# State-space rounds: two buffers for the cosine and sine tables, angles rounded on ScalarE one step sooner, two more chunks of the strips kept for the last round

## The chip, the cores and the metric

One Trainium2 chip, one core of it. The metric is the device time of one execution in microseconds (us). The kernel before was run three times; its time is the median. One more execution was recorded with the hardware profiler, and every row of the profile shown here is from that execution.

The engines are called as the profile calls them: PE (TensorE matmuls), PEld (its weight loads), DVE (VectorE), ACT (ScalarE), POOL (GpSimd) and SP (SyncE, which only starts transfers). The names with a q (SPq, ACTq, PEq) are the queues of instructions that start transfers or wait on semaphores.

## The reference, cut to what matters

A two-layer decoder trunk for 1024 tokens of width 1024, in float32. Layer 0 is a block-diagonal state-space mixer, layer 1 a forgetting attention. The change touches only the state-space mixer of layer 0:

```python
u, z = jnp.split(h @ w_in, 2, axis=-1)
abar = exp(ar*dt) * (cos(ai*dt) + i sin(ai*dt))        # 64 groups x 64 states
ug = u.reshape(bsz, L, 64, 16)                         # 64 groups of 16 channels
bu = einsum('blgc,gpc->blgp', ug, bb)                  # complex input of the states
s  = associative_scan(s_t = abar * s_{t-1} + bu_t)     # over the 1024 tokens, complex
y  = einsum('blgp,gcp->blgc', s_r, C_re) - einsum('blgp,gcp->blgc', s_i, C_im)
y  = gelu(y.reshape(bsz, L, 1024) + D * u)
y  = y * sigmoid(y @ w_glu + b_glu) * silu(z)
x  = x + gate * (y @ w_out)
```

## The kernel before, in words

**Layout of the scan.** Eight tokens make a chunk, so the scan runs over 128 chunks. The 64 groups are taken in eight rounds e = 0 to 7 of eight groups. A state tile is 128 partitions (64 real parts above 64 imaginary parts, or the reverse) by 8 groups by 128 chunks, which is 128x1024 in the profile. The complex recurrence is made real by turning the states by the angle of chunk k: the input is multiplied by cosine and sine (tables `cT` and `sT`), a real scan follows with a decay, and the result is turned back with the same tables.

**The functions of a round.**
- `products` (two halves, hb 0 and 1, of six DVE instructions each): builds the input matrix `wm` and the output matrix `moa` of a round. `moa` has two buffers, so that of round e+2 may be written only when PE has read that of round e in `states_out`.
- `turn_in` (PE transposes into `pin`, copied by ACT), `taps` (PE, `pk`), `toeplitz` (ACT copies into `kev`, then 8 small transfers on SP into `minb`), `load_u` (a transfer on SP).
- `states_in`: 16 matmuls into `vps`, copied by ACT into `v1`; `swap_halves` on ACT's queue makes `v2`, the same tile with its partition halves exchanged.
- `tables`: on DVE an add of the coarse and fine angle into `sT`, a `tensor_scalar` that rounds it into `cT` by adding and subtracting MAGIC (L521), a subtract that leaves the fraction of a turn in `sT`; then on ACT the absolute value and the cosine in `cT` and the sine in `sT`. One buffer each, so `tables` of round e+1 can't begin before `rotate_back` of round e is done.
- `scan`: two multiplications and an add on DVE into `r1`, the scan itself (L610) into the buffer of `v1`, then `swap_halves` on SP's queue. `rotate_back`: two multiplications and a subtract on DVE into `r1`; the second one needs the swapped tile.
- `states_out`: 32 matmuls (`py`, L628 and L629) that read `r1`, `moa`, `uu` and `minb`; ACT applies gelu into a tile `yb` (tag `r1`) and POOL starts its transfer into `y_d`. `r1` and `yb` alternate in two buffers, so `r1` of round e+1 also waits for the matmuls of round e; a memset on POOL (L605) opens it.

**Fill for PE.** Beside the rounds PE computes the strips of `h @ w_in` (u strips 4 to 7, z strips 0 to 7). A strip has a weight tile, split into a high part by ACT (`w_hi`, L93) and a low part by DVE (`w_lo`, L101), and three chunks of 24 matmuls (L264): one 258 columns wide, one of 512, one of 256. `unit(n)` puts the next n chunks into PE's order. There are 36 chunks: 5 stand ahead of round 0, three in each round, one more in each round with even e below 7 (e = 0, 2, 4, 6), and the last three after `states_out` of round 7.

**Order.** Two chains are written out by hand with `issue_after`: `ve` keeps the DVE work in program order (scan, products, rotate_back, tables, products of the round after next), `te` keeps the PE work. All else (which other instruction fills a gap, the order on ACT, SP and POOL) is set by a list scheduler when the program is built.

**After the rounds.** Eight loads `yl` (L715) bring y back from `y_d`. ACT and DVE split each half into a high and low part (L706, L707), into the same activation tiles that the z strips read, so these splits wait for the last z chunks. Then comes the GLU product `pj_g`, and all later stages of the layer and of layer 1.

Of the kernel before, what the change touches and what calls it, by code (L numbers as in the profile page):

```python
# [15 lines left out]
AF = mybir.ActivationFunctionType  # L16
ALU = mybir.AluOpType
# [17 lines left out]
MAGIC = 12582912.0  # L35
# [8 lines left out]
PI_LO = 3.1415925  # L44


def trunk(tc, a, out):
    nc = tc.nc
    V, S, G, T, Q = nc.vector, nc.scalar, nc.gpsimd, nc.tensor, nc.sync
    top = ExitStack()  # L50
    with top:
# [130 lines left out]
        with l0:  # L182
# [13 lines left out]
            def tt(o, x, y, op, eng=V):  # L196
                return eng.tensor_tensor(out=o, in0=x, in1=y, op=op).ins
# [4 lines left out]
            def halves(nm, top_v, bot_v):  # L202
                t = (tmp if nm[0] == "s" else s5).tile([P, 1], F32, name=nm, tag=nm)
                G.memset(t[0:64], top_v)
                G.memset(t[64:128], bot_v)
                return t

            sg_pm = halves("sg_pm", 1.0, -1.0)
            sg_mp = halves("sg_mp", -1.0, 1.0)
            tpi = halves("tpi", 2 * PI_LO, -2 * PI_LO)  # L210
            hpi = halves("hpi", math.pi / 2, math.pi / 2)
            e32 = float(np.float32(math.e))
            ecorr = (math.e - e32) / e32
# [58 lines left out]
            for k in range(KT):  # L272
# [3 lines left out]
                if k < 2:  # L276
                    w01[k] = weight_strip(a["a_w_in"][k], [P, KT, P])
                V.scalar_tensor_tensor(out=s_a[:, k:k + 1], in0=mod[:, 8 + k:9 + k], scalar=sc1[:, k:k + 1], in1=ga[:, k:k + 1],
                                       op0=ALU.add, op1=ALU.mult)
                for i in range(2):  # L280
# [3 lines left out]
                                           op0=ALU.mult, op1=ALU.subtract)  # L284
# [12 lines left out]
            for k in range(KT):  # L297
# [5 lines left out]
                                                 op0=ALU.add, op1=ALU.subtract).ins  # L303
# [90 lines left out]
            ylo = s5.tile([P, NG, 16], F32, name="ylo", tag="ylo")  # L394
            xhi = s5.tile([P, NG, 8], F32, name="xhi", tag="xhi")
# [30 lines left out]
            for m in (1, 2, 4):  # L426
                sh = [P, NG, m]
# [78 lines left out]
            def big(nm, bufs=2):  # L506
                return sb.tile([P, 8, NCH], F32, name=nm, tag=nm, bufs=bufs)
# [3 lines left out]
                    q.dma_start(out=o[64 * hh:64 * hh + 64], in_=x[64 - 64 * hh:128 - 64 * hh])  # L511


            def tables(e, st):

                cT, sT = st["tab"] = big("cT", 1), big("sT", 1)
                n8 = slice(8 * e, 8 * e + 8)
                sh = [P, 8, 8, 16]
                tt(sT.rearrange("p g (x y) -> p g x y", y=16), xhi[:, n8].unsqueeze(3).broadcast_to(sh),
                   ylo[:, n8].unsqueeze(2).broadcast_to(sh), ALU.add)  # L520
                V.tensor_scalar(out=cT, in0=sT, scalar1=MAGIC, scalar2=-MAGIC, op0=ALU.add, op1=ALU.add)  # L521
                end = tt(sT, sT, cT, ALU.subtract)
                S.activation(cT, sT, AF.Abs)
                S.activation(cT, cT, AF.Sin, scale=-2 * PI_LO, bias=hpi)
                S.activation(sT, sT, AF.Sin, scale=tpi)
                return end
# [47 lines left out]
            def toeplitz(e, st):  # L574

                pk = st["pk"]
                kev = sbm.tile([GC, 8, 8, GC], F32, name="kev", tag="kev", bufs=1)
                for q in range(4):
                    S.activation(kev[:, q:8:4].rearrange("c h m d -> c h (m d)"), pk[32 * q:32 * q + GC], AF.Copy)
                mi = minb[e % 2]  # L580
                for j in range(8):
                    Q.dma_start(out=mi[j:P:8, :, j:8, :], in_=kev[:, :, 0:8 - j, :])

            def load_u(e, st):
                st["uu"] = sb.tile([P, 8, NCH], F32, name="uu", tag="uu")
                loaded.append(Q.dma_start(out=st["uu"], in_=u_d[P * e:P * e + P].rearrange("(g c) j k -> (c j) g k", c=GC)).ins)
# [49 lines left out]
            loaded, sts, order = [], [{} for _ in range(KT + 2)], [None, None]  # L636
            strips = itertools.chain(*[u_strip(e) for e in range(U_FIRST, KT)], *[z_strip(e) for e in range(KT)])

            def behind(i):
                return ExitStack() if order[i] is None else tc.issue_after(order[i])  # L640


            def ve(f, *xs):
                with behind(0):
                    order[0] = f(*xs)

            def te(f, *xs):
                with behind(1):
                    order[1] = f(*xs)

            def unit(n=1):
                for _ in range(n):
                    te(lambda: next(strips, order[1]))
# [9 lines left out]
            te(taps, 0, 1, sts[0])  # L663
            te(states_in, 0, sts[0])
            unit()
            ve(tables, 0, sts[0])
            toeplitz(0, sts[0])
            ve(products, 1, 0, sts[1])
            unit()
            for e in range(KT):  # L670
                a_, b_, c_ = sts[e:e + 3]
                more = e + 1 < KT
                ve(scan, e, a_)
                unit()
                if more:
                    load_u(e + 1, b_)
                    te(turn_in, 0, b_)
                    te(taps, e + 1, 0, b_)
                    unit(2)
                    ve(products, e + 1, 1, b_)  # L680
                    te(turn_in, 1, b_)
                    te(taps, e + 1, 1, b_)
                    te(states_in, e + 1, b_)
                ve(rotate_back, a_)
                if more:
                    toeplitz(e + 1, b_)
                    ve(tables, e + 1, b_)
                if e % 2 == 0 or not more:
                    unit(1 if more else 2)
                if e + 2 < KT:  # L690
                    ve(products, e + 2, 0, c_)
                te(states_out, e, a_)
# [41 lines left out]
        with l0b:  # L734
# [38 lines left out]
            for e, i in OUT_SEQ:  # L773
# [8 lines left out]
                if sum(seen) and n < 40:  # L782
                    with tc.issue_after(xd):
# [3 lines left out]
                                       op0=ALU.mult, op1=ALU.add)  # L787
# [352 lines left out]
        for j, (n, c) in enumerate(steps):  # L1140
# [5 lines left out]
            p, h = n // 2, n % 2  # L1146
# [70 lines left out]
```

## Time and profile before

| | |
|---|---|
| time, median of 3 runs | 1225.78 us (1220.67 to 1227.47) |
| the profiled execution | 1223.69 us, span 1221.9 us |
| PE busy | 1162.0 us, 95% of the span |
| DVE busy | 848.9 us, 69% |
| ACT busy | 605.1 us, 50% |
| POOL busy | 367.8 us, 30% |
| granted PE clock over the span | 0.987 |
| rounds 0 to 7 | first scan instruction at 100.91 us, last matmul of the z strips at 299.08 us |

How to read it: busy shares are averages over stages with different limits, so a stage is read by its own windows and timelines. A row of a timeline gives the start, the duration, engine, line, operation, output and inputs, the shapes, and how often it stands there in sequence; in brackets stands the idle time of the engine just before it and what ended that. Matmuls overlap, so their step is the distance of two starts, not the duration.

### The profile page before, as it was taken

How to read it: one execution, taken by the hardware profiler on the slowest of the kernel's cores; microseconds unless marked ns; L12 is line 12 of the kernel's file. 1: busy time of each engine (PE TensorE's matmuls, PEld its weight loads, DVE VectorE, ACT ScalarE, POOL GpSimd, SP SyncE). 2: the span in 40 equal slices, each digit the busy share in tenths (PEclk: the TensorE clock that was granted, in tenths of full speed). 3: DMA queues.
4: the chain of work that ended last, by engine and by line, in shares of the span. 5: the costliest groups of instructions: out<-in, count | busy, mean ns of one | idle time of the engine just before them, and what ended most of it. 6: DMA issues, size and time to landing. Idle time of an engine off the chain costs nothing.

```text
span 1221.9 us, 20599 instructions
## 1 busy us (share of the span) xinstructions
PE 1162.0 (95%) x7542; PEld 1017.3 (83%) x7542; DVE 848.9 (69%) x1724; ACT 605.1 (50%) x1138; POOL 367.8 (30%) x568
## 2 busy tenths in 40 slices
PE   8989898997899998899989999999999999999898
PEld 6778887887778876799989989998888888888686
DVE  7889899874498767746444664448787778887421
ACT  6565766665335324322213452227677777886310
POOL 4000000000000033600133463447576666764100
PEclk9999999998989999999999999999999999999999
DMA  9754666584974885247543277518796968871242
GB/s 352 220 173 117 171 169 164 154 233 126 334 249 129 281 312 167 90 154 233 200 148 139 83 214 152 156 70 182 132 188 124 171 122 155 156 138 27 94 165 78
DMA packets 113333, 205.30 MB, mean 168 GB/s; under 512 B 17072, under 2 KB 58160, under 8 KB 111696
## 3 DMA queue, kind: packets, MB, share of 16 engines
q1 hardware_dynamic: 86272, 161.44, 41.4%
q0 software_dynamic: 24960, 37.75, 18.1%
q10 hardware_dynamic: 2000, 4.79, 1.7%
q8 instruction: 60, 0.98, 0.3%
q14 instruction: 41, 0.34, 0.1%
HBM read 146.47 MB, written 46.20 MB: 158 GB/s over the span
## 4 chain that ended last, share of the span: by engine, by line
PE 57%; DVE 16%; DMA 12%; ACT 5%; issue 5%; SPq 2%; POOL 2%; ACTq 0%; POOLq 0%; DVEq 0%
PE tkps L851 16%; PE zb L112 7%; PE pj_f L112 5%; PE tp L1043 5%; DMA modw<-modw 4%; PE u L264 4%; PE ov L1049 3%; PE ov L1050 3%; PE sp L1010 3%; DMA v_d<-vt 3%; PE sp L1011 3%; PE pj_g L112 2%; DMA mwx<-modw 2%; PE f L112 2%; DVE w_lo L101 1%
## 5 line engine op out<-in xcount | busy, mean ns | idle before, releaser
L851 PE MATMUL tkps<-wvh,aH 128*128 128x256 f32 (+1 forms) x768 | 220.5, 287 | 7.3 <-DVE vt L863 4.0
L851 PE MATMUL tkps<-wvh,aL 128*128 128x256 f32 (+1 forms) x768 | 217.1, 283 | 1.4 <-DVE aL L167 1.4
L851 PE MATMUL tkps<-wvl,aH 128*128 128x256 f32 (+1 forms) x768 | 216.7, 282 | 0.0
L851 PEld LDWEIGHTS tkps<-wvh,aH 128*128 128x128 f32 x768 | 145.2, 189 | 9.8 <-DVE vt L863 4.9
L851 PEld LDWEIGHTS tkps<-wvh,aL 128*128 128x128 f32 x768 | 145.1, 189 | 2.1 <-DVE aL L167 1.8
L851 PEld LDWEIGHTS tkps<-wvl,aH 128*128 128x128 f32 x768 | 145.3, 189 | 0.3 <-issue 0.2
L1045 ACT ACTIVATE pth<-tp 128x512 fp32r<-128x512 f32 (+1 forms) x192 | 87.2, 489 | 61.4 <-PE ov L1049 34.7
L1018 ACT ACTIVATE pr<-pr,mx 128x128 f32<-128x128 f32 (+7 forms) x128 | 98.9, 773 | 22.4 <-DVE mx L1015 21.8
L1020 POOL TENSOR_SCALAR pr<-pr,sm 128x128 f32<-128x128 f32 (+7 forms) x128 | 96.2, 761 | 40.6 <-DVE sm L1019 40.5
L1046 DVE TENSOR_TENSOR ptl<-tp,pth 128x512 fp32r<-128x512 f32 (+1 forms) x192 | 101.3, 551 | 9.0 <-ACT pth L1045 8.6
L93 ACT ACTIVATE w_hi<-w_raw 128x1024 fp32r<-128x1024 f32 x49 | 51.6, 1053 | 86.4 <-PE pj_f L112 29.5
L1015 DVE CUSTOM_DVE_ANT_0 pr<-sp,fb 128x512 f32<-128x512 f32 (+3 forms) x128 | 72.8, 569 | 21.3 <-PE tp L1043 19.9
L1049 PE MATMUL ov<-pth,vhl 128*128 128x256 f32 x320 | 85.6, 299 | 0.1
L1043 PE MATMUL tp<-ident,pr 128*128 128x128 f32 x576 | 82.9, 273 | 0.0
L874 ACT ACTIVATE hsq<-tkps 128x256 f32<-128x256 f32 x64 | 24.6, 384 | 117.8 <-PE tkps L851 112.5
L132 DVE CUSTOM_DVE_ANT_0 modw<-modw,c_b 128x1024 f32<-128x1024 f32 x48 | 58.6, 1223 | 34.0 <-DMA modw<-modw 33.7
L1050 PE MATMUL ov<-ptl,vhl 128*128 128x256 f32 x320 | 81.0, 286 | 0.2 <-DVE ptl L1046 0.2
L1010 PE MATMUL sp<-kk,qs 128*128 128x256 f32 (+2 forms) x192 | 74.5, 388 | 2.2 <-DVE mx L1015 1.9
L1043 PEld LDWEIGHTS tp<-ident,pr 128*128 128x128 f32 x576 | 65.3, 140 | 7.1 <-POOL pr L1020 0.5
L794 POOL TENSOR_TENSOR sq<-sq,sq 128x512 f32<-128x512 f32 x12 | 19.0, 1585 | 173.3 <-ACT sq L790 173.3
L877 POOL TENSOR_TENSOR hms<-hms,nhalf 128x4 f32<-128x4 f32 x64 | 67.6, 1057 | 5.0
L876 POOL TENSOR_SCALAR hms<-hms 128x4 f32<-128x4 f32 x64 | 15.2, 237 | 176.3 <-DVE hms L875 172.4
(325 smaller groups left out, 3305.4 us busy)
## 6 DMA issues: line engine op xcount, KB each, us to landing
modw<-modw SPq DMA_DIRECT2D x48, 512.0 KB, 5.1
kk<-k_d POOLq DMA_DIRECT2D x32, 512.0 KB, 6.8
wvr<-kvq_w SPq DMA_DIRECT2D x12, 1024.0 KB, 5.5
mwx<-modw SPq DMA_DIRECT2D x16, 512.0 KB, 7.5
w_raw<-a_w_in SPq DMA_DIRECT2D x16, 512.0 KB, 5.2
v_d<-vt SPq DMA_DIRECT2D x32, 256.0 KB, 2.5
fb<-f_d SPq DMA_DIRECT2D x16, 512.0 KB, 8.9
vhl<-v_d POOLq DMA_DIRECT2D x16, 512.0 KB, 9.7
```

Of the source, the lines that this page charges most:

```text
L112: T.matmul(ps, w[wt][:, k, :], act[at][k][half], start=(k == k0 and n == 0), stop=(k == k1 and n == 2))
L851: T.matmul(ps[:, 0:nv], at, wt[:, k, 0:nv], start=(n == 0), stop=(n == 3 * KT - 1))
L877: G.tensor_tensor(out=ms, in0=ms, in1=nhalf, op=ALU.pow)
L1010: T.matmul(sp[:, 0:wm_], qsl, kk[:, 0, lo:lo + wm_], start=True, stop=False)
L1015: V.tensor_tensor_reduce(out=pr[:, lo:hi], in0=sp[:, 0:w_], in1=fb[:, lo:hi], scale=1.0, scalar=3e38 if m0 is None else m0, op0=ALU.add, o ...
L1018: S.activation(pr[:, 0:nk], pr[:, 0:nk], AF.Exp, scale=-1.0, bias=mx, accum_out=sm)
L1020: G.tensor_scalar(out=pr[:, 0:nk], in0=pr[:, 0:nk], scalar1=sm, scalar2=0.0, op0=ALU.mult, op1=ALU.add)
L1043: T.transpose(out=tp[:, b, :], in_=prs[qi][:, P * (b0 + b):P * (b0 + b) + P], identity=ident)
L1045: S.activation(pth[:, 0:m, dst], tp[:, 0:m, :], AF.Copy)
L1046: V.tensor_tensor(out=ptl[:, 0:m, dst], in0=tp[:, 0:m, :], in1=pth[:, 0:m, dst].bitcast(F32), op=ALU.subtract)
L1049: T.matmul(ov, vhl[:, b, :], pth[:, b - b0, :], start=(b == 0), stop=False)
L1050: end = T.matmul(ov, vhl[:, b, :], ptl[:, b - b0, :], start=False, stop=(b == nb - 1)).ins
```

## The change

- `tables` is cut in two. `turns(e+1)` does the add into `sT` on DVE, then ACT writes the rounded angle into `cT`: an Identity activation with the tile `magic` as bias, so that float32 rounds the sum to a whole number plus MAGIC. It stands right behind `scan(e)` in the DVE chain. `tables` then does one DVE instruction, (cT - MAGIC) - sT into `sT`, and the same three activations as before; the sign of the sine's scale `tpi` is reversed, since the fraction now has the other sign. It stands ahead of `rotate_back(e)` instead of behind it.
- `cT` and `sT` get two buffers each (8 KB more in each partition). The scratch for POOL's transfer descriptors is set to 8192 bytes a partition; before it was left at its default.
- The extra chunk in even rounds is now put only into rounds with e divisible by 4 (e = 0 and 4). So 31 chunks stand ahead of `states_out` of round 7 and five after it, instead of 33 and three.

```diff
-            tpi = halves("tpi", 2 * PI_LO, -2 * PI_LO)
+            tpi = halves("tpi", -2 * PI_LO, 2 * PI_LO)
+            magic = halves("magic", MAGIC, MAGIC)
...
-            def tables(e, st):
-
-                cT, sT = st["tab"] = big("cT", 1), big("sT", 1)
+            def turns(e, st):
+
+                cT, sT = st["tab"] = big("cT"), big("sT")
                 n8 = slice(8 * e, 8 * e + 8)
                 sh = [P, 8, 8, 16]
-                tt(sT.rearrange("p g (x y) -> p g x y", y=16), xhi[:, n8].unsqueeze(3).broadcast_to(sh),
-                   ylo[:, n8].unsqueeze(2).broadcast_to(sh), ALU.add)
-                V.tensor_scalar(out=cT, in0=sT, scalar1=MAGIC, scalar2=-MAGIC, op0=ALU.add, op1=ALU.add)
-                end = tt(sT, sT, cT, ALU.subtract)
+                end = tt(sT.rearrange("p g (x y) -> p g x y", y=16), xhi[:, n8].unsqueeze(3).broadcast_to(sh),
+                         ylo[:, n8].unsqueeze(2).broadcast_to(sh), ALU.add)
+                S.activation(cT, sT, AF.Identity, bias=magic)
+                return end
+
+            def tables(st):
+
+                cT, sT = st["tab"]
+                end = V.scalar_tensor_tensor(out=sT, in0=cT, scalar=-MAGIC, in1=sT, op0=ALU.add, op1=ALU.subtract).ins
                 S.activation(cT, sT, AF.Abs)
...
-            ve(tables, 0, sts[0])
+            ve(turns, 0, sts[0])
+            ve(tables, sts[0])
...
                 ve(scan, e, a_)
                 unit()
                 if more:
+                    ve(turns, e + 1, b_)
                     load_u(e + 1, b_)
...
                     te(states_in, e + 1, b_)
+                    ve(tables, b_)
                 ve(rotate_back, a_)
                 if more:
                     toeplitz(e + 1, b_)
-                    ve(tables, e + 1, b_)
-                if e % 2 == 0 or not more:
+                if e % 4 == 0 or not more:
                     unit(1 if more else 2)
...
-    nc = bacc.Bacc("TRN2", target_bir_lowering=False, num_devices=1)
+    nc = bacc.Bacc("TRN2", target_bir_lowering=False, num_devices=1, dynamic_dma_scratch_size=8192)
```

## The prediction

> **What bounds the kernel now.** The page comes first: PE is busy nearly all the time, so what the change can win is idle or slowed PE time. Then the windows by stage (length, busy us and instruction count of PE, PEld, DVE, ACT, POOL, then clock, DMA share, GB/s), one per round, and the end of the rounds.
>
> ```profile
> PE 1162.0 (95%) x7542; PEld 1017.3 (83%) x7542; DVE 848.9 (69%) x1724; ACT 605.1 (50%) x1138; POOL 367.8 (30%) x568
> ...
> 100.90:129.20 28.30, 28.01 (x212) 25.39 (x210) 24.41 (x31) 17.58 (x25) 0.12 (x1) 1.00 0.50 129
> 174.50:196.50 22.00, 20.36 (x154) 18.11 (x153) 20.83 (x25) 15.38 (x26) 0.65 (x2) 1.00 0.67 182
> ...
> 268.00:280.00 12.00, 6.22 (x41) 5.49 (x39) 5.86 (x6) 4.01 (x6) 0.53 (x1) 0.90 0.89 258
> 280.00:290.00 10.00, 8.21 (x46) 8.24 (x47) 2.75 (x3) 1.20 (x2) 0.53 (x1) 0.61 0.27 88
> ```
>
> Round 0 (100.9 to 129.2) is full on PE. Round 3 (174.5 to 196.5) is not: PE lacks 1.6 us, DVE 1.2 us. The last round leaves PE idle for 5.8 and 1.8 us and then runs it at clock 0.61. Why, the DVE timeline says:
>
> ```profile
> 174.50 1.22 DVE L197 TENSOR_TENSOR r<-cT,v 128x1016 f32<-128x1016 f32 x1 [0.66 <-ACT cT L524]
> 187.44 1.23 DVE L197 TENSOR_TENSOR r<-r,sT 128x1024 f32<-128x1024 f32 x1
> 188.70 1.23 DVE L197 TENSOR_TENSOR sT<-xhi,ylo 128x1024 f32<-128x1024 f32 x1
> 189.96 0.69 DVE L521 TENSOR_SCALAR cT<-sT 128x1024 f32<-128x1024 f32 x1
> 190.69 1.23 DVE L197 TENSOR_TENSOR sT<-sT,cT 128x1024 f32<-128x1024 f32 x1
> 191.83 0.18 DVE L197 TENSOR_TENSOR dd<-dsk,idg 128x32 f32<-128x32 f32 x1
> 196.54 1.22 DVE L197 TENSOR_TENSOR r<-cT,v 128x1016 f32<-128x1016 f32 x1 [0.87 <-ACT cT L524]
> 219.07 0.69 DVE L197 TENSOR_TENSOR moa<-x1m,pwr 128x512 f32<-128x512 f32 x1 [2.55 <-PE py L629]
> 220.40 1.21 DVE L197 TENSOR_TENSOR r<-cT,v 128x1016 f32<-128x1016 f32 x1
> 265.91 1.22 DVE L197 TENSOR_TENSOR r<-cT,v 128x1016 f32<-128x1016 f32 x1 [4.52 <-ACT cT L524]
> 269.61 2.29 DVE L610 TENSOR_TENSOR_SCAN v<-dT,r 128x1024 f32<-128x1024 f32 x1
> 279.16 1.23 DVE L197 TENSOR_TENSOR sT<-sT,v 128x1024 f32<-128x1024 f32 x1 [6.00 <-DMA v<-v]
> 280.42 1.22 DVE L197 TENSOR_TENSOR r<-r,sT 128x1024 f32<-128x1024 f32 x1
> ```
>
> DVE goes through its hand-written chain without a pause: scan to the end of `rotate_back` is 174.50 to 188.67, 14.17 us; the tables take 188.70 to 191.83, 3.13 us; then products, and a scan that waits for the cosine. One round is 196.54 - 174.50 = 22.04 us. The row at 219.07 is a wait for PE: `moa` needs the matmuls of `states_out`. In the last round scan(7) waits 4.52 us for the cosine and `rotate_back` 6.00 us for its swap. PE's own timeline at those places:
>
> ```profile
> 191.79 0.39 PE L629 MATMUL py<-r,moa 128*128 128x128 f32 x2
> 218.64 0.39 PE L629 MATMUL py<-r,moa 128*128 128x128 f32 x2
> 262.07 0.39 PE L629 MATMUL py<-r,moa 128*128 128x128 f32 x2
> 281.79 0.77 PE L629 MATMUL py<-r,moa 128*128 128x128 f32 x2 [7.58 <-DVE r L197]
> 287.76 0.41 PE L264 MATMUL z<-aH,w_hi 128*128 128x258 f32 x1
> 290.78 0.39 PE L264 MATMUL z<-aH,w_hi 128*128 128x512 f32 x1
> 299.08 0.28 PE L264 MATMUL z<-aH,w_lo 128*128 128x256 f32 x1
> ```
>
> From here: `states_out` takes 188.67 to 192.18 = 3.51 us after its input; of the last strip the 258 wide chunk takes 3.0 us (287.76 to 290.78) and the 512 and 256 wide ones 8.6 together (to 299.08 + 0.28 = 299.4), 11.6 in all.
>
> **The change part by part.**
>
> *Tables on DVE.* Out go 1.26 + 0.73 + 1.14 = 3.13 us behind `rotate_back`; in come an add (1.26) and a fused subtract. For the latter no 128x1024 row exists; by the two-input row at 190.69 it is 1.14 to 1.23, by 128x512 rows of the fused form (below) up to 1.36. I take 1.14, so 2.4 us, now ahead of `rotate_back`. What it saves, 0.7 us, is not what decides; the place is.
>
> ```profile
> L758 DVE SCALAR_TENSOR_TENSOR zs<-zt,biz,zs 128x512 f32<-128x512 f32 x16 | 11.9, 744 | 0.0
> L524 ACT ACTIVATE cT<-cT,hpi x8: 1107/1149/1153, 99.8 to 264.7; 128x1024 f32<-128x1024 f32 x8
> ```
>
> *Rounding on ACT.* One more activation with a bias tile, 1.15 us by the L524 row, between `turns` and `tables`. DVE covers it with one half of products (the other half, 191.83 to 196.54 less the wait of 0.87, takes 3.8 us). ACT is busy 15.4 of 22 us in round 3, so it costs nothing unless an instruction ahead of it in ACT's queue waits for PE; then DVE stands at `tables` with `rotate_back` and PE's `states_out` behind it: 0 to 2 us a round, I take 0.
>
> *Two buffers, tables earlier.* The cosine is ready long before the next scan, so the waits of 0.66, 0.87 and 4.52 us go. Next late is `moa`: after `rotate_back` DVE has only dd, wm, tm, wm, tm (2.5 us: the 3.8 of a half less 1.33 for the two `moa`, 219.07 to 220.40) to do while PE needs 3.51 us. So a round without a spare chunk becomes a loop: end of `states_out` to scan, 220.40 - 219.03 = 1.37; scan to end of `rotate_back`, 14.17 + 2.4; `states_out`, 3.51. Sum 21.45 us (before: 22.04).
>
> *Chunks.* A round's own PE work is 11.6 of chunks, 3.5 of `states_out`, and the transposes, taps and `states_in`:
>
> ```profile
> 92.03 0.60 PE L557 MATMUL pin<-ident,wm 128*128 128x128 f32 x4
> 93.16 2.03 PE L594 MATMUL vps<-uu,min__963 128*128 128x128 f32 x16
> 94.94 0.37 PE L264 MATMUL u<-aH,w_hi 128*128 128x258 f32 x1
> 137.58 0.68 DVE L323 TENSOR_TENSOR et<-u,q2x 128x512 f32<-128x512 f32 x1
> ```
>
> That is 2.9 for the second half (92.03 to 94.94) and 1.1 for the first, 19.1 us together: below 21.45, so rounds 1, 2, 3, 5, 6 follow the loop. Round 4 keeps an extra chunk, now the 258 wide one: 19.1 + 3.0, about 22.4 with a short wait for taps. Round 1 also holds the last u strip's normalization on DVE: 0.6 for the 512 wide chunk (row above) and half of that twice for the others, 1.1 to 1.2 in all. Round 0 stays, PE being full.
>
> *Sum.* Rounds 1 to 6 took 125.5 to 262.4 (last `py` row at 262.07), 136.9 us. New: 22.5 + 4 x 21.45 + 22.4 = 130.7, so `states_out` of round 6 ends at 256.2. Scan(7) has no `moa` ahead of it: 256.4, ended 6.0 us later (265.91 to 271.9) at 262.4. Then the swap:
>
> ```profile
> 256.70 11.39 SPq L582 DMA_DIRECT2D minb<-kev  x8
> 271.93 1.14 SPq L511 DMA_DIRECT2D v<-v  x2
> DMA to landing us min/median/max: 3.1/3.7/8.3
> ```
>
> It landed after 7.2 us before, behind y loads and a weight load; from 3.1 to 8.3 is possible, I take 4.5. With 2.5 of DVE, `states_out` of round 7 can start at 269.6. PE is there at 256.2 + 11.6 + 0.6 (the first four `py`) = 268.4 and waits; `states_out` ends at 273.1, then come five chunks, 2 x 8.6 + 3.0 = 20.2: z ends at 293.3 instead of 299.4, **6.1 us earlier**. With the fastest swap PE sets it: 292.1. With the slowest the gap is 5 us, `states_out` runs at half clock as from 281.79 to 287.76 (6.0 us), and z ends at 299.5.
>
> *Two terms that I can't place.* A `w_lo` (1.14 us steps) lies within the 14.17; put into the `moa` wait it shortens a round by up to 1: 0 to -5 in five rounds. And PE now waits 21.45 - 19.1, about 2.3 us, ahead of each `states_out`. What a gap of that size costs, a later stage shows, with the windows behind it:
>
> ```profile
> 557.22 0.39 PE L851 MATMUL tkps<-wvh,aH 128*128 128x256 f32 x1 [2.11 <-DVE vt L863]
> 558.00:560.00 2.00, 2.00 (x12) 2.00 (x11) 2.00 (x5) 0.72 (x2) 0.00 (x0) 0.50 0.98 365
> 560.00:562.00 2.00, 2.00 (x15) 2.00 (x15) 2.00 (x3) 0.00 (x0) 0.00 (x0) 0.77 1.17 271
> ```
>
> Some 3 us at half clock, so 1.6 us lost; 0 to 8 in five rounds. I take two rounds of each: -2 and +3.2. The gain is then 6.1 - 1.2 = 4.9 us. If such gaps cost no clock at all, it is 8.1 and the time 1215.6, the low end of my forecast's own range, with 0.15 of its chance.
>
> The Trainium skill, "TensorE: Matmul & The Clock Gate", section "Why this matters for your kernels", asks for no PE gaps above about 3 us; by it 2.3 us would be harmless, which is that low end. The rows above differ from it, and I go by them.
>
> *At nothing.* The smaller descriptor scratch: PE's list of waits names no transfer of POOL's, so they are hidden; if the ring filled, head loads (row) would come later, with two steps of lookahead as cover. Bounds 0 and +3.
>
> ```profile
> kk<-k_d POOLq DMA_DIRECT2D x32, 512.0 KB, 6.8
> 336.35 0.79 PE L112 MATMUL pj_g<-aH,w_hi 128*128 128x512 f32 x1 [3.50 <-ACT sg L760]
> ```
>
> The stall in the GLU stage hangs on loads that follow the z strips, so it moves along unchanged.
>
> The profiled execution took 1223.69 us, span 1221.9 and 1.8 around it: 1223.69 - 4.9 = 1218.8. The median shown is 2.1 us above it; I forecast 1219.
>
> **The rivals.**
> 1. *The wait for `moa` is filled* by `w_lo` and the rest, and PE's gaps shrink with it to 1.2 us, so no clock is lost. Rounds of 20.5: 5 us more, gain 11, 1213. For it: the scheduler fills DVE's idle time. Against: in round 3 `w_lo` stood within products.
> 2. *The gain is eaten.* If `moa` is placed ahead of the second wm and tm, these 1.4 us (the larger part of the 2.5) stand behind the wait: 5 x 1.4 = 7 us, or the swap lands as late as before. Gain 0, 1224. For it: DVE's order is fixed ahead of the run, and the swap's 7.2 us is measured.
> 3. *Slower: PE cools down in every round.* `tables` and `rotate_back` now stand between products and `states_out`. If the rounding is 1.2 us late, PE's gap is 3.5 us, the wait in row 336.35, after which the window below shows clock 0.50: `states_out` takes 6.0 instead of 3.5. That is 3.7 x 5 = 18 us; with the two chunks behind, z ends near 311, +12: 1236. It decides where `states_out` of round 7 ends later than 287.8 - 8.6 = 279.2, since two chunks are now behind it.
>
> ```profile
> 336.00:338.00 2.00, 1.65 (x4) 1.36 (x5) 2.00 (x5) 1.24 (x2) 0.00 (x0) 0.50 0.98 298
> ```
>
> **How the numbers follow.** My forecast (1215 to 1222) has 0.45, rival 1 0.20, rival 2 0.22, rival 3 0.13. The range, 1209 to 1227, leaves out most of rival 3 and the far end of rival 1, under 2 in 10. A difference of 0.5%, 6.1 us, is about what a measurement can tell from none. The forecast lies at that bound: half of it, 0.22, and rival 1 make 0.42 faster; the other half and rival 2 make 0.45 the same; rival 3 is 0.13 slower.
>
> **What would show it.** Right: no wait for cT ahead of the scans, waits of about 1 us of `moa` on `py` in rounds 1 to 6, scan(7) near 256, `states_out` of round 7 near 270, z's end near 293, and the same distance from there to the end. Wrong: DVE waiting for the rounded cT, clock below 1.00 in the rounds, `states_out` of round 7 ending after 279, or later stages longer than before.

## The result, and the profile after

The kernel with the change took **1232.62 us** (median of 14 runs) against 1224.51 us for the kernel before on the same chip: ratio **1.0063, 95% interval 1.0047 to 1.0078**, so about 8 us slower. The forecast was 1219 us, and its range ended at 1227: it was wrong in size and in sign. The profiled execution after has a span of 1229.4 us (before: 1221.9).

First the page's line of engines, then windows of the kernel after, by round (length, then busy us and count of PE, PEld, DVE, ACT, POOL, then clock, DMA share, GB/s). The rows are rounds 1, 2, 3 and 6, each from about the end of one `states_out` to the next.

```profile
PE 1167.2 (95%) x7542; PEld 1023.3 (83%) x7542; DVE 844.7 (69%) x1716; ACT 614.1 (50%) x1146; POOL 369.8 (30%) x570
...
125.40:149.60 24.20, 21.00 (x150) 18.95 (x150) 21.50 (x28) 18.41 (x27) 0.90 (x2) 0.93 0.61 171
149.60:172.60 23.00, 21.14 (x151) 19.11 (x150) 20.05 (x24) 15.66 (x24) 0.66 (x2) 0.93 0.55 141
172.60:193.90 21.30, 19.45 (x150) 17.41 (x149) 20.05 (x24) 14.85 (x25) 0.65 (x2) 1.00 0.58 152
...
238.40:262.50 24.10, 21.40 (x152) 19.23 (x151) 17.77 (x19) 18.11 (x27) 0.76 (x3) 0.93 0.82 224
```

PE has as many matmuls as before and is busy 5.2 us longer. In rounds 1, 2 and 6 about 150 matmuls take 21.0 to 21.4 us at clock 0.93; in round 3 the same number takes 19.45 us at clock 1.00. The last `py` row of round 6 starts at 261.78, so `states_out` ends at 262.2, about where it ended before (262.5). Now the timeline of DVE after:

```profile
149.76 0.69 DVE L197 TENSOR_TENSOR moa<-x1m,pwr 128x512 f32<-128x512 f32 x1 [2.62 <-PE py L635]
194.02 0.69 DVE L197 TENSOR_TENSOR moa<-x1m,pwr 128x512 f32<-128x512 f32 x1 [0.99 <-PE py L635]
...
255.81 1.23 DVE L197 TENSOR_TENSOR r<-r,sT 128x1024 f32<-128x1024 f32 x1
267.48 1.22 DVE L197 TENSOR_TENSOR v<-sT,v 128x1016 f32<-128x1016 f32 x1 [10.44 <-DMA v<-v]
...
278.24 1.23 DVE L197 TENSOR_TENSOR sT<-sT,v 128x1024 f32<-128x1024 f32 x1 [3.52 <-DMA v<-v]
```

No scan waits for the cosine any more; DVE waits for PE at `moa` instead. But scan(7), which waited 4.52 us for the cosine before, now waits **10.44 us for its input swap**, a transfer that the prediction never priced. The rows of the queues say why: the swap is issued on ACT's queue (the first row is the copy that makes its input), while SP has started loads of y and the small transfers of `toeplitz`.

```profile
255.11 1.09 ACT L601 ACTIVATE v<-vps 128x512 f32<-128x512 f32 x2
257.89 0.47 ACTq L512 DMA_DIRECT2D v<-v  x1
259.75 0.47 ACTq L512 DMA_DIRECT2D v<-v  x1
...
249.15 2.53 SPq L723 DMA_DIRECT2D yl<-y_d  x2
...
256.35 11.96 SPq L588 DMA_DIRECT2D minb<-kev  x8
```

The list of transfers between 250 and 268 us (KB of each, then us from issue to landing) gives the swap 8.1 us in the kernel before (first row) and 7.9 us after (second), with loads of y of 512 KB beside it in both. The last row here is how ACT's queue started the swap in the kernel before:

```profile
v<-v ACTq DMA_DIRECT2D x2, 256.0 KB, 8.1
...
v<-v ACTq DMA_DIRECT2D x2, 256.0 KB, 7.9
yl<-y_d SPq DMA_DIRECT2D x4, 512.0 KB, 7.3
...
256.88 2.10 ACTq L511 DMA_DIRECT2D v<-v  x2
```

Before, the swap was issued from 256.9 on; 8.1 us later it is 265 to 266, just when the wait for the cosine ended (265.91): one wait hid the other. In the kernel after, its second half was also issued late, at 259.75, though the copy had ended at 256.2. Last, PE's timeline after:

```profile
144.74 0.50 PE L635 MATMUL py<-r,moa 128*128 128x128 f32 x2 [3.02 <-DVE r L197]
145.03 0.64 PE L634 MATMUL py<-uu,minb 128*128 128x128 f32 x2
...
167.68 0.46 PE L635 MATMUL py<-r,moa 128*128 128x128 f32 x2 [1.86 <-DVE r L197]
...
190.62 0.46 PE L635 MATMUL py<-r,moa 128*128 128x128 f32 x2 [1.85 <-DVE r L197]
190.92 0.39 PE L634 MATMUL py<-uu,minb 128*128 128x128 f32 x2
...
257.18 0.46 PE L635 MATMUL py<-r,moa 128*128 128x128 f32 x2 [2.29 <-DVE r L197]
...
280.87 0.77 PE L635 MATMUL py<-r,moa 128*128 128x128 f32 x2 [6.95 <-DVE r L197]
...
305.77 0.39 PE L112 MATMUL pj_g<-aH,w_hi 128*128 128x512 f32 x1
```

Behind the gap of 3.02 us a `py` row (two matmuls) takes 0.64 us instead of 0.39; behind those of 1.86 and 2.29 the rows become as slow about a microsecond later. `states_out` of round 7 starts at 280.87, 0.9 us earlier than before (281.79). But five chunks stand behind it instead of three, so the first `pj_g` starts at 305.77 instead of 299.20: +6.6 us, nearly all of the span's +7.5.

### The profile page after: what moved, and what is told of

It reads as the page before. It is cut to its first block, busy times and chain, and to the rows that moved or that the text cites. A ratio compares the mean times of both kernels' runs of the same rounds, so it can differ in the third digit from the quotient of the medians.

```text
span 1229.4 us, 20587 instructions
## 1 busy us (share of the span) xinstructions
PE 1167.2 (95%) x7542; PEld 1023.3 (83%) x7542; DVE 844.7 (69%) x1716; ACT 614.1 (50%) x1146; POOL 369.8 (30%) x570
## 4 chain that ended last, share of the span: by engine, by line
PE 63%; DVE 12%; DMA 12%; ACT 5%; issue 4%; SPq 2%; POOL 1%; POOLq 0%; ACTq 0%; DVEq 0%
PE tkps L859 14%; PE zb L112 7%; PE pj_f L112 5%; PE tp L1051 5%; PE pj_g L112 5%; PE pj_o L112 4%; PE z L265 4%; DMA modw<-modw 3%; PE ov L1057 3%; PE ov L1058 3%; DMA v_d<-vt 3%; PE sp L1018 3%; PE u L265 2%; PE sp L1019 2%; DMA v<-v 2%
## 5 line engine op out<-in xcount | busy, mean ns | idle before, releaser
L1026 ACT ACTIVATE pr<-pr,mx 128x128 f32<-128x128 f32 (+7 forms) x128 | 98.9, 773 | 22.7 <-DVE mx L1023 21.9
```

Source lines behind the costliest of these rows:

```text
L1026: S.activation(pr[:, 0:nk], pr[:, 0:nk], AF.Exp, scale=-1.0, bias=mx, accum_out=sm)
```

## The experiments

Two theories stood after the result. **Theory 1:** the transfers hold scan(7), `states_out` of round 7 doesn't come earlier, and the two chunks moved behind it are pure loss; half clock in the rounds takes the rest. **Rivals:** the tables themselves, or the smaller descriptor scratch, make the rounds slower. The first four kernels shared runs of the kernel before with a median of 1223.74 us, the next four 1224.44, the last two 1223.78. "First `pj_g`" below is the start of its first matmul, where the z strips have ended.

**1. The tables alone** (the change, with the chunks left where they were):

```diff
-                if e % 4 == 0 or not more:
+                if e % 2 == 0 or not more:
```

> The change's tables alone (two buffers, rounding on ACT, tables ahead of rotate_back, smaller scratch), with the extra chunks where they were before (e = 0, 2, 4, 6). Theory 1 (the two chunks moved behind states_out of round 7 are what costs, because that states_out is set by the late swaps of the last round and doesn't come earlier): states_out of round 7 still begins near 281, z ends near 281 + 5.5 + 11.6 = 298, time about 1223, level with before. Theory 2 (the new place of tables makes the rounds themselves longer through PE gaps and half clock): rounds 1 to 6 end no earlier than 262 and the time stays at 1229 or more. Theory 3 (the smaller scratch or a new order later on costs): time stays near 1232 with z ending before 300.

Measured: 1225.89 us, ratio 1.0018 (0.9995 to 1.0042). Timeline of DVE, then of PE:

```profile
266.26 1.23 DVE L101 TENSOR_TENSOR w_lo<-w_raw,w_hi 128x1024 fp32r<-128x1024 f32 x1 [6.16 <-ACT w_hi L93]
270.48 1.22 DVE L197 TENSOR_TENSOR v<-sT,v 128x1016 f32<-128x1016 f32 x1 [3.00 <-DMA v<-v]
...
283.86 0.77 PE L635 MATMUL py<-r,moa 128*128 128x128 f32 x2 [3.95 <-DVE r L197]
300.90 0.39 PE L112 MATMUL pj_g<-aH,w_hi 128*128 128x512 f32 x1
```

The tables neither win nor lose: the interval holds 1. The cosine is early, and scan(7) waits for the swap all the same; here a `w_lo` split, which the scheduler placed ahead of it, waits 6.16 us as well.

**2. The chunks alone** (the kernel before, with the opposite edit):

```diff
-                if e % 2 == 0 or not more:
+                if e % 4 == 0 or not more:
```

> The kernel before with the extra chunk only in rounds 0 and 4, nothing else changed. Theory 1: states_out of round 7 begins near 280 to 282 as before, with PE waiting about 4 us longer ahead of it, and five chunks behind it: z ends at about 280 + 6 + 20.2 = 306, time about 1231. Theory 2: the chunks are harmless: rounds get shorter by what is taken out, time 1222 to 1225. Theory 3: as theory 2, 1224.

Measured: 1232.41 us, ratio 1.007 (1.0049 to 1.0091): the loss of the whole change, from this part alone.

```profile
262.18 1.22 DVE L197 TENSOR_TENSOR r<-cT,v 128x1016 f32<-128x1016 f32 x1 [4.42 <-ACT cT L524]
...
277.81 0.76 PE L629 MATMUL py<-r,moa 128*128 128x128 f32 x2 [8.03 <-DVE r L197]
302.18 0.39 PE L112 MATMUL pj_g<-aH,w_hi 128*128 128x512 f32 x1
```

Taking two chunks (8.6 us) out of the rounds brings `states_out` of round 7 only 4.0 us forward, because DVE and transfers set it; PE stands idle 8.03 us there, and the chunks come behind. The first `pj_g` is 3.0 us late. The time rose by 8.7 us: the rest lies in later stages that the edit doesn't touch. The stretch from the first `pj_g` to the end is 930.0 us here and 922.7 in the kernel before, and it ranged from 920.2 to 933.1 over the profiles of this study. At most 2.0 us of it can be placed (see what stays open, below).

**3. The descriptor scratch alone** (the kernel before; every engine's instructions stay in the same order):

```diff
-    nc = bacc.Bacc("TRN2", target_bir_lowering=False, num_devices=1)
+    nc = bacc.Bacc("TRN2", target_bir_lowering=False, num_devices=1, dynamic_dma_scratch_size=8192)
```

> The kernel before with the descriptor scratch of 8192 bytes; every engine's order is that of before. Theories 1 and 2: 1224.5, no difference. Theory 3: 1228 to 1232, with longer waits on POOL's transfers in the attention.

Measured: 1223.95 us, ratio 0.9997 (0.998 to 1.0013). Nothing. As its order is that of the kernel before, its profile also shows what one execution differs from another by: its first `pj_g` starts at 300.52 instead of 299.20. Differences of a microsecond or two between single profiles prove nothing here.

**4. The changed kernel with the loads of y held back** until the last swap has been issued:

```diff
-                with tc.issue_after(loaded[-1]):
+                with tc.issue_after(swapped[-1]):
                     last_y = Q.dma_start(out=yls[k], in_=y_rows(k)).ins
```

(`swapped` collects the swaps issued on SP's queue.)

> The changed kernel with the y loads held on SP's queue until the last swap of rotate_back is issued (before: until the last u load). Theory 1, with the y loads as what delays the swaps of the last round: the swap for scan(7), issued at 258 to 260, lands near 263 instead of 267.5; scan(7) ends near 268.5, its own swap lands after 3.7 instead of 4.7 us, states_out of round 7 begins near 275 instead of 281, z ends near 299 to 300 instead of 306: time about 1225 to 1227. If the eight small minb transfers and not the y loads hold the swaps up, nothing moves: 1231 to 1233. If the later y loads are late for the splits, PE waits behind the z strips and it is as slow or slower.

Measured: 1227.81 us, ratio 1.0029 (1.0007 to 1.005). A row of the list of transfers, then ACT's copy and its queue, DVE, and PE:

```profile
v<-v ACTq DMA_DIRECT2D x2, 256.0 KB, 4.1
...
254.38 1.09 ACT L603 ACTIVATE v<-vps 128x512 f32<-128x512 f32 x2
255.50 1.13 ACTq L512 DMA_DIRECT2D v<-v  x2
...
260.99 1.22 DVE L197 TENSOR_TENSOR v<-sT,v 128x1016 f32<-128x1016 f32 x1 [5.31 <-DMA v<-v]
...
274.46 0.76 PE L637 MATMUL py<-r,moa 128*128 128x128 f32 x2 [3.50 <-DVE r L197]
300.19 0.39 PE L112 MATMUL pj_g<-aH,w_hi 128*128 128x512 f32 x1
```

With no load of y beside it the swap lands in 4.1 us instead of 7.9, scan(7) begins 6.5 us earlier, `states_out` of round 7 6.4 us earlier and `pj_g` 5.6 us earlier. Both halves are also issued right behind the copy, within 1.13 us. So it is the loads of y that make the swap late, through its start and its landing; what exactly held back the start isn't shown. (The hold also lets a store of z and a weight load, which stood among the loads of y on SP's queue, start earlier; the runs don't separate them from y.) The 6.5 us aren't all the swap's: DVE was ready 1.4 us earlier here, at 255.7, and the wait shrank by 5.1 us. Yet scan(7) still waits 5.31 us, since the swap can't be issued before ACT's copy has ended, at 255.47. The time, 1227.8, is a little above the 1225 to 1227 expected.

**5. The kernel before with the same hold.**

> The kernel before, with the loads of y held on SP until the last swap is issued. Theory 1 (the loads of y are what makes the swaps of scan(7) land late): scan(7) itself does not move, because in this kernel it waits for the cosine (265.91, 4.52 us); its swap, issued at 271.9, lands after about 3.7 us instead of 7.2; the wait ahead of the product with the sine at 279.16 falls from 6.00 to 2.5 us; states_out(7) starts at about 278 instead of 281.79; the first pj_g moves from 299.20 to about 296, and the time is 3 us lower, about 1221. Rival (the swap is slow for another reason): the wait stays near 6 us, and the time is that of the kernel before, 1224, or more, because the y loads now come later and the GLU stage waits for them.

Measured: 1219.64 us, ratio 0.997 (0.9949 to 0.9991).

```profile
268.21 1.22 DVE L197 TENSOR_TENSOR r<-cT,v 128x1016 f32<-128x1016 f32 x1 [4.53 <-ACT cT L526]
...
281.58 0.77 PE L631 MATMUL py<-r,moa 128*128 128x128 f32 x2 [4.83 <-DVE r L197]
298.07 0.39 PE L112 MATMUL pj_g<-aH,w_hi 128*128 128x512 f32 x1
```

The hold helps the kernel before too. Scan(7) still waits for the cosine there (4.53 us), and it was 2.3 us later in this kernel. The wait for the swap behind that scan fell from 6.00 to 3.49 us (2.5 was expected), so `states_out` of round 7 hardly moved (281.58, not 278), and the first `pj_g` starts 1.1 us earlier (3 expected). The time fell by 4.8 us all the same, by the medians; where the rest was won isn't shown.

**6. The tables with the hold, chunks as before** (experiments 1 and 4 together).

> The table part of the change with the chunks as they were before, and the loads of y held on SP until the last swap is issued. Theory 1: scan(7) waits for neither the cosine nor its input swap for long (under 5.5 us, from about 261), states_out(7) starts at 274 to 277 instead of 283.86 without the hold, three chunks follow, the first pj_g starts at 292 to 295 instead of 299.20, and the time is 1218 to 1221. Rival (the hold costs as much later, the y loads being late for the GLU stage): the first pj_g starts early as said, but the stall in the GLU stage grows by the same 4 to 7 us, and the time is 1223 to 1226.

Measured: **1218.19 us, ratio 0.9952 (0.993 to 0.9973)**, faster than the kernel before and the kernel after. Against experiment 5, the hold without the change, it is only 1.5 us less, and the two intervals overlap: that the tables add to what the hold wins is not shown by the time.

```profile
264.94 1.23 DVE L101 TENSOR_TENSOR w_lo<-w_raw,w_hi 128x1024 fp32r<-128x1024 f32 x1 [4.66 <-ACT w_hi L93]
...
279.53 0.46 PE L637 MATMUL py<-r,moa 128*128 128x128 f32 x2 [3.07 <-DVE r L197]
295.65 0.39 PE L112 MATMUL pj_g<-aH,w_hi 128*128 128x512 f32 x1
```

`pj_g` starts 3.6 us earlier than in the kernel before and 2.4 earlier than in experiment 5, though `states_out` of round 7 starts later than I had expected (279.5 rather than 274 to 277): a `w_lo` split stands ahead of scan(7) and waits 4.66 us for its `w_hi`, which ACT writes behind cosine and sine.

**7. Fill for PE's gaps**, to test the half clock: the kernel of experiment 4 with matmuls of ones ahead of `states_out`; they read `onesm` and their product is overwritten.

```diff
                     py = s5ps.tile([P, 4, P], F32, name="py", tag="py", bufs=2)
+                    for _ in range(14 if hb == 0 and e in (1, 2, 3, 5, 6) else 0):
+                        T.matmul(py[:, 0, :], onesm, onesm, start=True, stop=True)
```

> The changed kernel with the loads of y held as in after_hold, and with 14 matmuls of ones ahead of the matmuls of states_out in rounds 1, 2, 3, 5 and 6, whose product is overwritten: they fill about 1.6 us of the time in which PE waits for r1. Theory (the half clock in rounds 1 and 2 comes from the idle gap of PE): the gaps of 3.02 and 1.85 us shrink by 1.6 us, states_out of rounds 1 and 2 takes 3.5 us instead of 4.9, and the last states_out row of round 6 comes 2 to 3 us earlier than 258.81. Time 1.5 to 3 us below after_hold's 1227.8. Rival (the half clock comes from something else, the load on the chip for one): states_out of these rounds stays at 4.9 us and round 6 ends where it did, time 1227 to 1229.

Measured: 1228.85 us, ratio 1.0051 (1.0028 to 1.0074): no gain. Windows of rounds 1 and 2, and the fill on PE in round 3:

```profile
125.60:148.20 22.60, 22.40 (x178) 20.46 (x178) 21.41 (x28) 16.89 (x26) 0.90 (x2) 1.00 0.59 162
148.20:170.60 22.40, 22.40 (x178) 20.52 (x178) 20.07 (x25) 16.44 (x26) 0.65 (x2) 1.00 0.57 162
...
186.05 3.29 PE L635 MATMUL py<-onesm 128*128 128x128 f32 x28
```

The clock is 1.00 in both rounds, and round 1 is 1.6 us shorter than in experiment 4 (24.2). But each matmul of ones stands in the trace as two (14 give x28), so the fill takes 3.29 us, twice what I had meant: PE is now full in rounds 1 to 3, and rounds 3, 5 and 6, which had lost no clock, became 1.1, 1.4 and 1.2 us longer.

**8. Other rounds for the spare chunks** (experiment 6, with `e in (1, 2, 4, 5)` in place of `e % 2 == 0`).

> As tables_hold, but the four spare chunks stand in rounds 1, 2, 4 and 5 instead of 0, 2, 4 and 6, as many as before; three chunks stay behind states_out(7). Theory (round 0 is full on PE, so a chunk there costs its whole 4.3 us, and the other rounds have about 2 us of PE idle each): states_out of round 6 ends 2 to 4 us earlier than in tables_hold, and the time is 2 to 4 us lower, 1215 to 1218. Rival (PE's idle time in those rounds is only moved: a chunk in front of states_out makes moa and the next scan as much later): no difference from tables_hold beyond 1 us.

Measured: 1221.0 us, ratio 0.9972 (0.9945 to 0.9998): no better than experiment 6. DVE, then PE:

```profile
262.62 1.22 DVE L197 TENSOR_TENSOR r<-cT,v 128x1016 f32<-128x1016 f32 x1 [3.60 <-PE py L637]
...
278.79 0.77 PE L637 MATMUL py<-r,moa 128*128 128x128 f32 x2 [4.52 <-DVE r L197]
296.15 0.39 PE L112 MATMUL pj_g<-aH,w_hi 128*128 128x512 f32 x1
```

The 2.2 us won by round 6 (its last `py` row at 262.14, in experiment 6 at 264.33) were lost again in the last round: PE's gap ahead of `states_out` grew from 3.07 to 4.52 us, and the half clock began at once instead of a microsecond later.

**9. Half the fill, in the two rounds that lost clock in experiment 4** (experiment 7 with 7 matmuls, in rounds 1 and 2 alone).

> As after_hold, with 7 matmuls of ones ahead of states_out in rounds 1 and 2 alone. In after_hold_warm 14 of them took 3.3 us of PE (28 steps of 0.117), so that they filled more than the gap; 7 take 1.65 us. Theory (the half clock of rounds 1 and 2 comes from PE's idle gap): the gaps of 3.02 and 1.85 us become 1.4 and 0.2, the clock of both rounds is 1.00, round 1 takes 22.6 us and round 2 about 21.5 instead of 24.2 and 22.9, and states_out of round 6 ends 2 to 3 us earlier than 258.81; time 1225 to 1226, against 1227.8. Rival (the half clock comes from what runs beside it): rounds 1 and 2 as in after_hold, time 1227 to 1229.

Measured: 1227.23 us, ratio 1.0034 (1.0018 to 1.0051). Windows of rounds 1 and 2, then PE:

```profile
124.40:147.00 22.60, 20.95 (x164) 18.91 (x163) 21.37 (x29) 16.89 (x26) 0.89 (x2) 1.00 0.59 158
147.00:168.50 21.50, 21.22 (x166) 19.18 (x165) 20.24 (x25) 15.56 (x25) 0.66 (x2) 1.00 0.59 162
...
187.33 0.46 PE L639 MATMUL py<-r,moa 128*128 128x128 f32 x2 [2.69 <-DVE r L197]
```

Rounds 1 and 2 did what the theory of the gap said (22.6 and about 21.5): 22.6 and 21.3 us from last `py` row to last `py` row, at clock 1.00. Then the gain was given back: round 3 had a gap of 2.69 us, fell to half clock and took 24.3 us, so that the last `py` row of round 6 came only 0.5 us earlier (258.34) than in experiment 4, and the time missed the 1225 to 1226 expected.

**10. Experiment 6 with 7 matmuls of ones in round 1 alone.**

> As tables_hold, with 7 matmuls of ones ahead of states_out in round 1 alone, where PE's gap is 3.02 us and the first py steps behind it take 0.77 instead of 0.39. Theory (gap, then half clock): round 1 (125.2 to 150.6 in tables_hold) shortens from 25.4 to about 22.6 us, and all behind it starts 2 to 3 us earlier as far as no transfer holds it: time 1215 to 1217. Rival (the half clock has another cause, or the wait for the w_hi of the strip ahead of scan(7) takes the gain back): states_out(7) starts where it did, time 1218.

Measured: **1216.24 us, ratio 0.9936 (0.9915 to 0.9958)**, the fastest kernel of the study, though its interval overlaps that of experiment 6.

```profile
144.98 0.46 PE L639 MATMUL py<-r,moa 128*128 128x128 f32 x2 [1.46 <-DVE r L197]
...
292.62 0.39 PE L112 MATMUL pj_g<-aH,w_hi 128*128 128x512 f32 x1
```

PE's gap is 1.46 us instead of 3.02, round 1 takes 22.6 us instead of 25.4, and the first `pj_g` starts 3.0 us earlier than in experiment 6 and 6.6 earlier than in the kernel before. (The profiled execution took 1223.25 us, the longest of the ten.)

## Why the prediction was wrong, point by point

- **The step that failed: "Scan(7) has no `moa` ahead of it: 256.4".** It took away the wait for the cosine and asked only whether `moa` was next late, not whether the input swap was: that wait was put at nothing, and no reason was given. Measured: DVE was ready at 257.0 and scan(7) began at 267.48. Experiment 4 splits these 10.4 us: about 5.1 go when the loads of y are held back, and 5.3 stay, the swap's own time, as it can't start before `states_in(7)` has been copied. The row was there to be read in the kernel before: 8.1 us for the swap on ACT's queue, issued from 256.9 on.
- **The sum of rounds 1 to 6, 130.7 us, measured 136.7** (125.5 to 262.2). The loop itself was right where PE kept its clock: round 3 took 21.3 us (said: 21.45), round 5 21.9, round 4 22.5 (22.4). The term for half clock was mis-sized: its price per event was right (1.6 us each), but three rounds paid it, not two, and those three (24.2, 22.9 and 23.75 us) are 1.7, 1.5 and 2.3 us above the 22.5 and 21.45 said. The counter-term, `w_lo` in the wait for `moa` for -2 us, did not show.
- **The swap behind scan(7), taken at 4.5 us, took 4.75** (issued at 273.49, read from 278.24). Right.
- **`states_out` of round 7 at 269.6: measured 280.87,** 11.3 late, and at half clock behind a gap of 6.95 us, so that it ended at 286.2 instead of 273.1. The five chunks then took 19.6 us (said: 20.2). z's end is 305.8 instead of 293.3: 12.5 us late, nearly all of the 13.6 by which the forecast missed the time.
- **Right:** no wait for the cosine, about 1 us of `moa` on `py` where the clock is full, no wait of DVE for the rounding on ACT in rounds 1 to 6, the fused subtract at a step of 1.14 us, as taken (251.67 to 252.81), nothing for the descriptor scratch (0.9997).
- **The rivals.** Rival 3 had the right point of decision: slower if `states_out` of round 7 ends after 279.2. It ended 7.0 us after, and the first `pj_g` is 6.6 us late. Its mechanism, a late rounding on ACT in every round, was wrong; a transfer put it there. Rival 2 named the swap as slow as before, but thought of the one behind the scan.
- **The skill's rule.** The Trainium skill, "TensorE: Matmul & The Clock Gate", section "Why this matters for your kernels", asks for no idle gaps of PE above about 3 us between bursts of matmuls. By that rule shorter gaps would be harmless; behind the gaps of 1.86 and 2.29 us (rows 167.68 and 257.18) `states_out` took 1.6 us longer all the same, as the prediction held against it.

What stays open: why kernels with the two chunks behind `states_out` of round 7 lose more in time than at the first `pj_g` (8.7 against 3.0 us in experiment 2; in experiment 9 a loss of 0.34%, about 4 us, though the first `pj_g` starts 0.6 us earlier, at 298.63, in a profiled execution that was 3 us shorter than the median of its runs). One wait can be named: where the attention of layer 1 begins, PE's `sp`, its first product, waits 1.0 to 2.0 us for a load of `qs` on POOL's queue in each of the five kernels with five chunks there (2.0 in experiment 2, 1.0 in the kernel after), and 0.3 us or nothing in the seven with three. It isn't the smaller descriptor scratch, which experiment 2 doesn't have. Why the load comes late there, and where the rest goes, the runs don't show.

## What to carry to other kernels

When an edit removes a wait, list every input of the step that waited and when each arrived: the profile names only the last, and here a swap that landed together with the cosine was as late a bound as the cosine itself. Put more work behind a point only when something shows that this point comes earlier; first look which transfers share its moment, since holding back loads that nobody needed yet was worth more than the edit (0.997 for the hold alone, 1.0018 for the tables alone). Where an engine's idle time is filled, look at the rounds behind it too: the gain can come back as a longer gap there.

## What the runs showed of the hardware

Behind the gaps of rounds 1, 2 and 6 of the kernel after, a fall to half clock lasts 3.4 us each time. For round 1 the windows are these:

```profile
144.00:146.00 2.00, 1.26 (x7) 1.30 (x8) 1.97 (x5) 1.99 (x3) 0.00 (x0) 0.76 0.86 161
146.00:148.00 2.00, 2.00 (x11) 2.00 (x11) 1.11 (x2) 1.98 (x3) 0.00 (x0) 0.50 0.66 166
148.00:150.00 2.00, 2.00 (x18) 2.00 (x17) 0.24 (x1) 1.76 (x4) 0.11 (x1) 0.89 0.66 258
```

The clock is 0.76, 0.50 and 0.89, so 0.48 + 1.00 + 0.22 = 1.7 us are lost, which is 3.4 us at half; 168 to 174 (0.73, 0.50, 0.92) and 257 to 263 (0.67, 0.50, 0.98) give the same. The Trainium skill, "TensorE: Matmul & The Clock Gate", section "What's actually happening", gives a free-running window of 3413 ns, and the length agrees. Where PE had waited longer, the clock stayed down longer: around the gap of 7.58 us in round 7 of the kernel before it is 0.50 from 278 to 286.

What I had not expected is that the size of a gap doesn't decide alone. `states_out` takes 3.0 us from the first row behind the gap to its last at full clock, and 4.6 with such a fall in it: gaps of 1.85, 1.86, 2.29 and 2.69 us (166.54 in experiment 4; 167.68 and 257.18 after; 187.33 in experiment 9) gave 4.6, while other gaps of 1.85, 2.60 and 2.69 us (190.62 after; 275.59 in experiment 7; 259.17 in experiment 8) gave 3.0. All gaps of 3.0 us and more ahead of `states_out` cost it, none of 1.68 or less did. A window that runs by itself would explain the spread between, but not that a gap of 1.86 us, little more than half of its length, is enough; no run here tells on what it depends.

A small transfer suffers from its neighbours: the halves of the swap between partitions, 256 KB each, landed in 4.1 us with no load of y beside them (experiment 4) and in 7.9 us beside loads of 512 KB (kernel after), though those were issued by another engine. A store of z and a weight load stood beside it there too.
